# Two instead of three pairs of plain column tiles in each ConvFFN of a hybrid decoder trunk

## The chip, the cores and the metric

The kernel runs on one core of one Trainium2 chip. The metric is the device time of one execution in microseconds (us). The core has five engines that run side by side, each with its own queue worked off in order: TensorE (PE, matrix products; weight loads are shown as PEld), VectorE (DVE), ScalarE (ACT), GpSimd (POOL) and SyncE (SP, which here only issues transfers). They wait for one another by semaphores. Products land in eight PSUM banks, and DVE or ACT must take them out before a bank is used again.

## The reference

One step of a two-layer decoder trunk for 1024 prompt tokens and 8 x 8 sample tokens, 1088 columns in all, with 1024 channels. Layer 0 mixes tokens by sliding-window attention, layer 1 by a gated spatial MLP. Each layer ends with a ConvFFN, and this is what the change touches:

```
def conv_ffn(h, past, w_up, conv_w, conv_b, w_down):
    T = h.shape[1]
    a = h @ w_up
    ap = jnp.concatenate([past.astype(a.dtype), a], 1)
    conv = sum(conv_w[j] * ap[:, j:j + T] for j in range(CONV_W)) + conv_b
    g, u = jnp.split(conv, 2, axis=-1)
    y = (jax.nn.silu(g) * u) @ w_down
    return y, ap[:, T:]
```

Here h is the normalised and modulated input (1024 channels), w_up has 2 x 2816 columns, which are 2 x 22 tiles of 128, and each gate tile j belongs with the up tile 22 + j.

## The kernel before, in words

Activations are kept with channels on partitions and tokens along the row. Every float32 operand is split into a high part, rounded to the fast matmul type, and the remainder, so that a product needs three matmuls: high by high, high by low, low by high. The 1088 tokens lie in two halves h of 544, each of which has a first part of 272 (z = 0) and a second (z = 1).

**The norm** (class Norm4, line 1415) makes h in tiles `hf`, one for each z, group g of four channel blocks, and parity b. Lines 1450 and 1451 split them into `ha` and `hb` (16 tiles for the whole input). `sums` (line 1456) makes, for each of the four groups (z, g) in `todo`, the four block sums that the seven-product scheme needs, in four DVE instructions (lines 1459 to 1462) into two tiles `T`, after which the two `hf` tiles are free. `split` (line 1465) splits the two `T` into two `th` (ACT, line 1469) and two `tl` (DVE, line 1470).

**Plain columns.** For the first NCV = 3 pairs of column tiles (gate j and up 22 + j) the kernel takes plain products: `u_conv` (line 1654) and `u_step` (line 1512) run 8 channel blocks x 3 matmuls x 2 halves = 48 matmuls of 272 columns for each tile and z. They read `ha` and `hb` only, so PE has work while the sums are made. The first two columns start within the last block of the projection before (`last_block7`, line 1536), which also calls the weight splitter `ws.split` six times (lines 1554 and 1572); for a plain column that is an ACT cast (line 309) and a DVE subtraction (line 316) into two of the eight weight buffers, for raw weights of a seven-product pair only the load (lines 299 to 302). In `ffn` (line 1782) the second halves of three columns run interleaved while the norm's second part is applied (lines 1855 to 1860); the fourth column's follows, and the fifth and sixth run whole, in the loop at line 1869.

**Seven-product pairs.** The other 19 pairs use a Strassen-Winograd scheme over 2 x 2 blocks (channel parity by gate/up side against channel parity by token half): seven products in the order 1, 2, 4, 6, 5, 7, 3 (`pair`, line 1659), each 12 matmuls for each z, and DVE additions of the results (lines 1674 to 1704). Products 1, 2 and 3 read `ha` and `hb`; 4 to 7 read the split sums `th` and `tl`. `pair_weights` (line 1612) prepares the seven weights: each is an ACT cast (line 1621) and a POOL subtraction (line 1622); weights 1, 2 and 4 come straight from the raw blocks, 6 and 5 from the sums `Sa` (POOL, lines 1629 and 1632), 7 and 3 from `Sb` (lines 1636 and 1639). For the first pair, two steps of this (GA = 2) come ahead of the last plain half and the rest follow.

**Convolution and gate.** `conv` (line 1804) is one ACT pass (line 1807) and two DVE passes (lines 1808 and 1810) over 1104 columns into a tile `cv`; the last columns are saved by ACT for plain columns and by POOL for the others (lines 1812 to 1817). `gate` (line 1820) is ACT's SiLU, two DVE products (lines 1823 and 1824), a POOL copy (line 1825), and a store on ACT's queue.

**What sets the order.** The attention part is ordered by hand; from line 1187 on the framework's planner orders each engine's queue when the program is built: an instruction goes in when its inputs are ready by the planner's own estimate of times, earlier code first. Most large tiles come from one pool of 37 slots (NSLOT), and an instruction whose tile gets no slot waits. Weights have eight buffers, raw weights two.

In the loop over the plain columns n (tile n // 2, gate or up by n % 2), the work beside PE's is, in the order of the code: take out the column, convolve it, split whatever was summed, at n = 0 and 2 sum another group, at odd n the gate of the pair. Two groups are summed ahead of the loop, and the first of them is split there.

Of the kernel before, what the change touches and what calls it, by code (L numbers as in the profile page):

```python
# [33 lines left out]
GA, GB = 2, 0  # L34
STEPS = {4: (0, 2), 6: (1, 3), 7: (4, 6)}
RA, RB, RC = 0, 1, 7
NCV = 3
SLOT = 1106
SH1, SC1, G1, SH2, SC2, G2 = range(6)
ORD = (0, 2, 1, 3, 4, 6, 5, 7)  # L40
# [27 lines left out]
def plan():  # L68
# [25 lines left out]
    def ffn(l):  # L94
        r = []
        for j in range(NJ):
            if j < NCV:
                r += [(("up", l, j), 1024), (("up", l, NJ + j), 1024)]
# [242 lines left out]
def build(nc, tc, a, ctx):  # L341
# [15 lines left out]
    def banks(n, name="b"):  # L357
        return [bank(name) for _ in range(n)]
# [184 lines left out]
    with ExitStack() as p1:  # L543
# [102 lines left out]
        un2, yb, todo, done = [], {}, {}, []  # L646
# [965 lines left out]
    def pair_weights():  # L1612

        (_, l, j), r1, _ = ws.take("ua")
        r2 = ws.take("ub")[1]
        A11, A21, A12, A22 = r1[:, 0:512], r1[:, 512:1024], r2[:, 0:512], r2[:, 512:1024]
        W = {}

        def parts(i, src, eng=G):
            t = wp.tile([128, 1024], F32R, name="w7", tag="w")  # L1620
            A.copy(t[:, 0:512], src)  # L1621
            eng.tensor_sub(t[:, 512:1024], src, t[:, 0:512].bitcast(F32))  # L1622
            W[i] = t
        yield W
        parts(1, A11)
        yield
        parts(2, A12)
        sa = slot([128, 2, 512], name="Sa")
        G.tensor_add(sa[:, 0, :], A21, A22)
        yield  # L1630
        parts(4, A22)
        G.tensor_sub(sa[:, 1, :], sa[:, 0, :], A11)  # L1632
        yield
        parts(6, sa[:, 1, :])
        sb = slot([128, 2, 512], name="Sb")
        G.tensor_sub(sb[:, 0, :], A11, A21)
        yield
        parts(5, sa[:, 0, :])
        G.tensor_sub(sb[:, 1, :], A12, sa[:, 1, :])
        yield  # L1640
        del r1, r2, A11, A12, A21, A22, sa
        parts(7, sb[:, 0, :])
        yield
        parts(3, sb[:, 1, :])
        del sb
        yield
# [7 lines left out]
    def u_conv(norm, w, z, ps):  # L1654

        for k in ORD:
            u_step(norm, w, z, ps, k, k == 0, k == 7)
# [124 lines left out]
    def ffn(l, norm, nxt):  # L1782
# [6 lines left out]
        def ext(jj):  # L1789
            e = slot([128, 1106], name="ext")  # L1790
            es = e[:, 1026:1106].rearrange("p (b t) -> p b t", t=10)
            G.memset(e[:, 0:2], 0.0)
            G.tensor_copy(es[:, :, 0:2], past[:, jj])
            return e
# [9 lines left out]
        def conv(e, jj):  # L1804
            es = e[:, 1026:1106].rearrange("p (b t) -> p b t", t=10)
            t = slot([128, 1106], name="cv")
            A.activation(t[:, 0:1104], e[:, 2:1106], AF.Identity, scale=cw(jj * 3 + 2), bias=cb(jj))  # L1807
            V.scalar_tensor_tensor(t[:, 0:1104], e[:, 1:1105], cw(jj * 3 + 1), t[:, 0:1104],  # L1808
                                   op0=ALU.mult, op1=ALU.add)
            V.scalar_tensor_tensor(t[:, 0:1104], e[:, 0:1104], cw(jj * 3), t[:, 0:1104],  # L1810
                                   op0=ALU.mult, op1=ALU.add)
            if jj % NJ < NCV:
                A.copy(past[:, jj], es[:, :, 8:10])
                A.copy(stp[:, jj, :], e[:, 1024:1026])
            else:
                G.tensor_copy(past[:, jj], es[:, :, 8:10])
                G.tensor_copy(stp[:, jj, :], e[:, 1024:1026])
            return t

        def gate(j, tg, tu):  # L1820
            A.activation(tg[:, 0:1104], tg[:, 0:1104], AF.Silu)
            sv = [q[:, 1026:1106].rearrange("p (b t) -> p b t", t=10)[:, :, 0:8] for q in (tg, tu)]
            V.tensor_mul(tg[:, 0:SEQ], tg[:, 0:SEQ], tu[:, 0:SEQ])  # L1823
            V.tensor_mul(v88(tu[:, 0:64]), sv[0], sv[1])
            G.tensor_copy(tg[:, SEQ:T], tu[:, 0:64])
            A.dma_start(ps_scr[j], tg[:, 0:T])


        def evac(e, ps, z):
            for h in range(2):  # L1830
                for o, f in places(e, h, z):
                    A.copy(o, f(ps[h]))

        todo = [(z, g) for z in range(2) for g in range(2)]
# [25 lines left out]
                    u_step(norm, un[n], 1, bk[n], k, k == 0, k == 7)  # L1860
        w = un[3]
        un = None
        for g_ in range(2):
            norm.sums(*todo[0], V)
            taken.append(todo.pop(0))
            if not g_:
                norm.split(*taken.pop(0))
        ts = []
        for n in range(2 * NCV):
            jj = n % 2 * NJ + n // 2  # L1870
            if n < 3:
                e, ps = es[n], bk[n]
                es[n] = bk[n] = None
            else:
                if n == 3:
                    e = es.pop()
                else:
                    w = ws.take("up")[1:]
                    ps = banks(2, "u")
                    e = ext(jj)  # L1880
                    u_conv(norm, w, 0, ps)
                    evac(e, ps, 0)
                if n == 2 * NCV - 1:
                    gen = pair_weights()
                    W = next(gen)
                    for _ in range(GA):
                        next(gen)
                ps = banks(2, "u")
                u_conv(norm, w, 1, ps)
                if n == 2 * NCV - 1:  # L1890
                    for _ in range(GB):
                        next(gen)
                w = None
            evac(e, ps, 1)
            del ps
            ts.append(conv(e, jj))
            del e
            if n >= 2 and n < 2 * NCV - 2:
                ws.ahead(2)
            while taken:  # L1900
                norm.split(*taken.pop(0))
            if todo and n % 2 == 0:
                norm.sums(*todo[0], V)
                taken.append(todo.pop(0))
            if n % 2 == 1:
                gate(n // 2, *ts)
                ts = []
# [29 lines left out]
        return nn  # L1937

    norm = ffn(0, norm, lambda: Norm7(None, None, paired=True))


# [33 lines left out]
    todo = [(z, q) for z in range(2) for q in range(4)]  # L1975
# [155 lines left out]
    norm = Norm4(mods[1, SC2], mods[1, SH2])  # L2131
    down.run(norm, {LA: lambda: rest(0), LB: lambda: rest(1)})
    norm = ffn(1, norm, Norm)
    norm.finish()

# [27 lines left out]
```

## Time and profile before

| | |
|---|---|
| time, median of 3 runs | 2590.87 us (2586.61 to 2592.92) |
| the profiled execution's own time | 2589.49 us |
| its span, first to last instruction | 2587.7 us |
| mean granted TensorE clock | 0.994 |
| first ConvFFN: second half of the fourth plain column starts | 488.36 us |
| first ConvFFN: first seven-product pair starts | 518.47 us |
| matmuls | 17916 |

The profile is one execution. A row of the timeline reads: start in us, duration in us, engine, line of the code, operation, output <- inputs, shapes, how many instructions were merged into the row, and in square brackets how long the engine had been idle before and what released it. A row of the table of stages reads: the stretch, its length, busy us of PE, PEld, DVE, ACT and POOL with their instruction counts, then the granted clock (1.00 is full speed) and the transfers. Matmuls are pipelined: one of 272 columns lasts 0.288 us in the rows, but the next starts about 0.125 us after it.

### The profile page before, as it was taken

What the parts mean: (1) busy time and instruction counts of PE and PEld (TensorE: products, weight loads), DVE (VectorE), ACT (ScalarE), POOL (GpSimd) and SP (SyncE); (2) the same over time, 40 slices, a digit from 0 to 9 for tenths busy, and PEclk for the clock granted to TensorE, in tenths of its full rate; (3) what the DMA queues carried; (4) which work ended last, traced back from release to release, by engine and by line L of the source; (5) the groups of instructions that cost most, each with busy time, mean ns of one, the idle gap of its engine ahead of it and who ended that gap; (6) DMA issues with size and microseconds to landing.
All of it is one profiled execution on the core that took longest, in us unless ns stands there. A gap on an engine that the chain in (4) does not pass through costs nothing.

```text
span 2587.7 us, 45783 instructions
## 1 busy us (share of the span) xinstructions
PE 2535.6 (98%) x17916; PEld 2373.8 (92%) x17916; DVE 1616.8 (62%) x3254; ACT 982.6 (38%) x1939; POOL 1240.9 (48%) x1392
## 2 busy tenths in 40 slices
PE   7999999999999999999999999999999999999998
PEld 4667789999999999999788999999999999999998
DVE  5416866767767764456744555655687766676545
ACT  3216854533334331114325655212553333332203
POOL 2325631399999900001643755212179999940003
PEclk9999999999999999999999999999999999999999
DMA  8342214022222275453322534522112222254211
GB/s 302 102 153 100 74 57 139 10 80 81 85 81 76 93 288 181 159 187 127 91 84 76 169 127 156 200 99 74 66 59 76 76 80 79 77 192 158 89 45 70
DMA packets 113943, 292.20 MB, mean 113 GB/s; under 512 B 15328, under 2 KB 47136, under 8 KB 113696
## 3 DMA queue, kind: packets, MB, share of 16 engines
q1 hardware_dynamic: 82016, 232.49, 27.4%
q10 hardware_dynamic: 31712, 56.79, 5.8%
q8 instruction: 142, 2.33, 0.4%
q14 instruction: 73, 0.60, 0.1%
HBM read 228.06 MB, written 63.07 MB: 113 GB/s over the span
## 4 chain that ended last, share of the span: by engine, by line
PE 86%; DVE 6%; ACT 3%; POOL 2%; DMA 2%; issue 1%; SPq 0%; ACTq 0%; DVEq 0%; POOLq 0%
PE m L375 32%; PE acc L375 23%; PE misc L375 9%; PE v L375 7%; PE y L375 5%; PE u L375 5%; PE adaps L375 1%; POOL w L1622 1%; DMA raw<-wts 1%; ACT P L841 1%; PE rs L375 1%; DVE cv L1823 1%; PE pv L375 1%; DVE cv L1810 1%; PE sc L375 1%
## 5 line engine op out<-in xcount | busy, mean ns | idle before, releaser
L375 PE MATMUL m<-th,w 128*128 128x272 f32 x2944 | 562.6, 288 | 6.4 <-DVE ext L1676 6.3
L375 PEld LDWEIGHTS m<-th,w 128*128 128x128 f32 x2944 | 466.2, 188 | 7.0 <-issue 6.6
L375 PE MATMUL m<-tl,w 128*128 128x272 f32 x1472 | 424.9, 289 | 0.0
L536 DVE SCALAR_TENSOR_TENSOR x<-acc,mod,x 128x384 f32<-128x384 f32 (+1 forms) x312 | 159.6, 567 | 237.6 <-PE acc L375 232.0
L375 PE MATMUL m<-hb,w 128*128 128x272 f32 x2208 | 294.3, 289 | 0.0
L375 PEld LDWEIGHTS m<-hb,w 128*128 128x128 f32 x2208 | 285.1, 190 | 0.0
L375 PEld LDWEIGHTS m<-tl,w 128*128 128x128 f32 x1472 | 277.5, 189 | 0.0
L375 PE MATMUL acc<-gh,whi 128*128 128x384 f32 (+1 forms) x1152 | 255.9, 330 | 1.1 <-DVE mixed L2089 0.8
L375 PE MATMUL acc<-gl,whi 128*128 128x384 f32 (+1 forms) x1152 | 253.6, 328 | 0.6 <-DVE gl L1729 0.6
L375 PE MATMUL acc<-gh,wlo 128*128 128x384 f32 (+1 forms) x1152 | 253.2, 327 | 0.0
L309 ACT CAST whi<-raw 128x1024 fp32r<-128x1024 f32 (+1 forms) x108 | 109.7, 1017 | 377.9 <-PE acc L375 230.5
L1622 POOL TENSOR_TENSOR w<-raw,w 128x512 fp32r<-128x512 f32 x138 | 194.5, 1422 | 82.2 <-ACT w L1621 76.0
L375 PEld LDWEIGHTS acc<-gh,whi 128*128 128x128 f32 x1152 | 194.7, 188 | 10.2 <-issue 6.2
L375 PEld LDWEIGHTS acc<-gl,whi 128*128 128x128 f32 x1152 | 195.6, 188 | 0.9 <-DVE gl L1729 0.9
L1808 DVE SCALAR_TENSOR_TENSOR cv<-ext,cst,cv 128x1104 f32<-128x1104 f32 x88 | 125.4, 1460 | 112.9 <-ACT cv L1807 53.9
L375 PEld LDWEIGHTS acc<-gh,wlo 128*128 128x128 f32 x1152 | 195.7, 188 | 0.0
L1621 ACT CAST w<-Sa 128x512 fp32r<-128x512 f32 x92 | 56.8, 622 | 307.9 <-POOL Sa L1632 162.0
L1676 DVE TENSOR_TENSOR ext<-ev,m 128x272 f32<-128x272 f32 (+1 forms) x456 | 137.5, 338 | 47.6 <-PE m L375 39.3
L1303 POOL TENSOR_TENSOR nsq<-nsq 128x544 f32<-128x544 f32 x18 | 24.9, 1385 | 273.4 <-ACT nsq L1296 273.4
L1810 DVE SCALAR_TENSOR_TENSOR cv<-ext,cst,cv 128x1104 f32<-128x1104 f32 x88 | 155.6, 1802 | 0.1
L375 PE MATMUL m<-ha,w 128*128 128x272 f32 x1104 | 146.6, 289 | 0.0
L375 PEld LDWEIGHTS m<-ha,w 128*128 128x128 f32 x1104 | 141.2, 188 | 0.6
(293 smaller groups left out, 5506.8 us busy)
## 6 DMA issues: line engine op xcount, KB each, us to landing
raw<-wts SPq DMA_DIRECT2D x238, 512.0 KB, 4.0
wada<-wts SPq DMA_DIRECT2D x54, 512.0 KB, 4.3
pscr<-cv ACTq DMA_DIRECT2D x44, 544.0 KB, 5.5
p<-pscr SPq DMA_DIRECT2D x40, 544.0 KB, 5.5
xscr<-x ACTq DMA_DIRECT2D x24, 512.0 KB, 2.8
x<-xscr SPq DMA_DIRECT2D x24, 512.0 KB, 8.3
sscr<-mixed ACTq DMA_DIRECT2D x16, 544.0 KB, 3.5
vscr<-v ACTq DMA_DIRECT2D x32, 256.0 KB, 2.6
```

What stands on the lines that cost most here:

```text
L309: nc.scalar.copy(hi[:, :c], r[:, :c])
L375: PE.matmul(out, lhsT=l, rhs=r, start=start, stop=stop)
L536: V.scalar_tensor_tensor(xv, p[:, 0:w], gp, xv, op0=ALU.mult, op1=ALU.add)
L841: A.activation(p, p, AF.Exp, bias=nm[:, h:h + 1], scale=0.125, accum_out=su[:, h:h + 1])
L1303: (V if z or m == 7 else G).tensor_add(s.ss[z], s.ss[z], q)
L1621: A.copy(t[:, 0:512], src)
L1622: eng.tensor_sub(t[:, 512:1024], src, t[:, 0:512].bitcast(F32))
L1676: V.tensor_add(o, f(p), f(q))
L1808: V.scalar_tensor_tensor(t[:, 0:1104], e[:, 1:1105], cw(jj * 3 + 1), t[:, 0:1104], op0=ALU.mult, op1=ALU.add)
L1810: V.scalar_tensor_tensor(t[:, 0:1104], e[:, 0:1104], cw(jj * 3), t[:, 0:1104], op0=ALU.mult, op1=ALU.add)
L1823: V.tensor_mul(tg[:, 0:SEQ], tg[:, 0:SEQ], tu[:, 0:SEQ])
```

## The change

NCV goes from 3 to 2, so that plain products make the first two pairs of column tiles and the seven-product scheme the other 20. Of the four groups of block sums, three instead of two are summed ahead of the loop, and the first two instead of the first are split there. Within the loop, the one that is left is summed after n = 1 instead of after n = 0 and n = 2. The order of the weights in memory, `plan` (line 68), follows NCV.

```
-NCV = 3
+NCV = 2
...
-        for g_ in range(2):
+        for g_ in range(3):
             norm.sums(*todo[0], V)
             taken.append(todo.pop(0))
-            if not g_:
+            if g_ < 2:
                 norm.split(*taken.pop(0))
         ts = []
         for n in range(2 * NCV):
...
             while taken:
                 norm.split(*taken.pop(0))
-            if todo and n % 2 == 0:
+            if todo and n % 2 == 1:
                 norm.sums(*todo[0], V)
                 taken.append(todo.pop(0))
             if n % 2 == 1:
                 gate(n // 2, *ts)
```

With NCV = 2 the loop has four columns, all of which have been started before it; the weights of the first pair are prepared at n = 3.

More of the change, by code (lines that the diff above doesn't have):

```diff
@@ L36 @@
 RA, RB, RC = 0, 1, 7
-NCV = 3
+NCV = 2
 SLOT = 1106
@@ L1862, in ffn @@
         un = None
-        for g_ in range(2):
+        for g_ in range(3):
             norm.sums(*todo[0], V)
             taken.append(todo.pop(0))
-            if not g_:
+            if g_ < 2:
                 norm.split(*taken.pop(0))
@@ L1901, in ffn @@
                 norm.split(*taken.pop(0))
-            if todo and n % 2 == 0:
+            if todo and n % 2 == 1:
                 norm.sums(*todo[0], V)
```

## The prediction

> **What bounds the kernel now.** I read the page's busy times first, then the table of stages around the first ConvFFN, then the queues of TensorE (PE), VectorE (DVE), ScalarE (ACT) and GpSimd (POOL) in order of time. The second ConvFFN runs the same way 1386.2 us later (the last two rows below, its first block sum), so one is worked out and doubled.
>
> ```profile
> span 2587.7 us, 45783 instructions
> PE 2535.6 (98%) x17916; PEld 2373.8 (92%) x17916; DVE 1616.8 (62%) x3254; ACT 982.6 (38%) x1939; POOL 1240.9 (48%) x1392
> 427.00:455.00 28.00, 24.40 (x168) 23.50 (x168) 20.52 (x49) 13.43 (x26) 0.00 (x0) 0.88 0.45 150
> 455.00:488.40 33.40, 33.40 (x267) 33.37 (x268) 19.29 (x28) 16.46 (x34) 6.49 (x17) 1.00 0.01 1
> 488.40:518.40 30.00, 30.00 (x241) 30.00 (x241) 28.96 (x25) 21.20 (x45) 13.89 (x10) 1.00 0.05 20
> 518.40:539.50 21.10, 21.10 (x170) 21.10 (x170) 16.37 (x24) 8.00 (x18) 19.50 (x18) 1.00 0.27 89
> 602.70:630.00 27.30, 24.57 (x183) 24.38 (x183) 19.07 (x26) 10.87 (x17) 27.22 (x30) 0.94 0.36 110
> 470.88 0.72 DVE L1459 TENSOR_TENSOR T<-hf 128x544 f32<-128x544 f32 x1
> 1857.06 0.72 DVE L1459 TENSOR_TENSOR T<-hf 128x544 f32<-128x544 f32 x1
> ```
>
> The columns after the stage and its length are busy us of PE, weight loads, DVE, ACT and POOL, then the granted clock and the DMA. PE is the bound: it never pauses from 455 to 602.7. But in the stretch where the plain columns end (488.4 to 518.4) DVE is also 97% busy, and in the pair stretch POOL is 92%. That is the stretch the change shortens.
>
> ```profile
> 488.36 0.67 PE L375 MATMUL u<-ha,whi 128*128 128x272 f32 x4
> 518.47 3.19 PE L375 MATMUL m<-ha,w 128*128 128x272 f32 x24
> 524.51 0.29 PE L375 MATMUL m<-th,w 128*128 128x272 f32 x1
> 539.54 3.18 PE L375 MATMUL m<-ha,w 128*128 128x272 f32 x24
> ```
>
> Row 488.36 starts the second half of the fourth plain column, 518.47 the first seven-product pair, 524.51 its third product (i=4, the first that reads the split block sums), 539.54 the next pair.
>
> **The change part by part.**
>
> *TensorE.* Removed per ConvFFN: one pair of plain columns, 2 columns x 2 halves x 48 = 192 matmuls. Added: one seven-product pair, 7 x 2 x 12 = 168. A pair takes 539.54 - 518.47 = 21.07 us, or 0.1254 us a matmul, so 24 fewer are worth 3.0 us; 6.0 us for both ConvFFNs, 0.23% of the time. Even whole, this is under the 0.3% (7.8 us) that a measurement of this kernel can tell from no change. The added pair also brings POOL some 19.5 us of work and DVE 16.4 (row 518.4); both are under PE's 21.07, so the pairs that follow stay PE's.
>
> *The block ahead.* The last block of the preceding projection calls the weight splitter six times. Now only four of the six find a plain column; the fifth and sixth find raw weights of the first pair and issue only the load. Gone there are two ACT casts and two DVE subtractions, and one cast stands in front of a wait of PE:
>
> ```profile
> 443.30 1.04 ACT L309 CAST whi<-raw 128x1024 fp32r<-128x1024 f32 x1 [1.48 <-PE misc L375]
> 445.20 1.22 DVE L316 TENSOR_TENSOR wlo<-raw,whi 128x1024 fp32r<-128x1024 f32 x1
> 445.49 0.53 PE L375 MATMUL u<-ha,whl 128*128 128x272 f32 x2 [1.98 <-ACT ha L1450]
> 446.82 0.82 PE L375 MATMUL u<-ha,whl 128*128 128x272 f32 x2 [0.81 <-ACT ha L1450]
> 449.27 4.49 PE L375 MATMUL u<-ha,whl 128*128 128x272 f32 x20
> 492.63 0.68 ACT L1621 CAST w<-raw 128x512 fp32r<-128x512 f32 x1
> ```
>
> The weight buffer that the cast waited for now goes to a cast of the first pair's weights. The planner does pull those forward: row 492.63 is one, though the code has it after the sixth column's first half. So I exchange 1.04 for 0.68 and take 0.4 us. Bounds: 0; and 2.79 us (both waits) plus what 20 matmuls took over 20 x 0.1254 there, 4.49 - 2.51 = 1.98, so 4.8.
>
> *Sums and splits.* The third group's sum and the second group's split move ahead of the first convolution, where DVE has a hole:
>
> ```profile
> 478.03 0.72 DVE L1462 TENSOR_TENSOR T<-hf,T 128x544 f32<-128x544 f32 x1
> 489.15 1.37 DVE L1808 SCALAR_TENSOR_TENSOR cv<-ext,cst,cv 128x1104 f32<-128x1104 f32 x1 [10.39 <-ACT cv L1807]
> 490.44 1.29 DVE L1470 TENSOR_TENSOR tl<-T,th 128x1088 fp32r<-128x1088 f32 x1
> 491.64 1.37 DVE L1810 SCALAR_TENSOR_TENSOR cv<-ext,cst,cv 128x1104 f32<-128x1104 f32 x1
> 492.92 1.29 DVE L1470 TENSOR_TENSOR tl<-T,th 128x1088 fp32r<-128x1088 f32 x1
> 503.84 2.31 DVE L1823 TENSOR_TENSOR cv<-cv 128x1024 f32<-128x1024 f32 x1
> 506.07 1.35 DVE L1808 SCALAR_TENSOR_TENSOR cv<-ext,cst,cv 128x1104 f32<-128x1104 f32 x1
> 508.77 0.75 DVE L1459 TENSOR_TENSOR T<-hf 128x544 f32<-128x544 f32 x1
> 511.77 1.37 DVE L1808 SCALAR_TENSOR_TENSOR cv<-ext,cst,cv 128x1104 f32<-128x1104 f32 x1 [0.22 <-ACT cv L1807]
> 515.55 1.28 DVE L1470 TENSOR_TENSOR tl<-T,th 128x1088 fp32r<-128x1088 f32 x1
> ```
>
> A split costs two tl of 1.2 us (start to start), a sum 2.8 us (508.77 to 511.77, less the idle 0.22): 5.2 us into a hole of 10.39. Free, if slots suffice: 16 tiles of the norm, 4 columns, 4 weight parts, 8 split sums, 2 sums and 2 unsummed ones are 36 of the 37. Otherwise the sum falls behind 489.15 and adds 2.8 to the next step.
>
> *The fourth group.* It is still summed between convolutions, after the second, and split after the third. The first convolution cannot start earlier, since 488.36 does not move. But the first pair moves from 518.47 to 488.36 + 48 x 0.1254 = 494.4, 24.1 us earlier. Its i=4 product then starts at 524.51 - 24.1 = 500.4, and wants the fourth group in the last quarter, 18 matmuls later, at 502.7. DVE's list from 489.15 until that split is done: three convolutions of 2.6 (489.15 to 490.44 and 491.64 to 492.92), two splits of 2.4, the sum 2.8, the first gate product 2.2 (503.84 to 506.07): 17.6 us, so 506.8, with no waits. The old list (four convolutions, three splits, two sums, one gate product, 25.4 us) took 27.7 us to 516.83, so waits of up to 2.3 come on top. PE waits 4.1 to 6.4 us; I take 5. If the planner put the split ahead of the gate product and the third convolution (4.8 us), nothing would be left; the rows show it following the code.
>
> *Weights of the first pair.* The first three weights read raw data and can be made ahead, in the gap that POOL has. The next four need the sums Sa and Sb, which take slots:
>
> ```profile
> 493.39 3.87 POOL L1622 TENSOR_TENSOR w<-raw,w 128x512 fp32r<-128x512 f32 x1 [30.24 <-ACT w L1621]
> 515.79 2.18 POOL L1629 TENSOR_TENSOR Sa<-raw 128x512 f32<-128x512 f32 x1 [2.59 <-DVE cv L1810]
> 518.05 2.15 POOL L1632 TENSOR_TENSOR Sa<-Sa,raw 128x512 f32<-128x512 f32 x1
> 523.11 1.30 POOL L1622 TENSOR_TENSOR w<-Sa,w 128x512 fp32r<-128x512 f32 x1 [1.45 <-ACT w L1621]
> 530.58 3.56 POOL L1622 TENSOR_TENSOR w<-Sb,w 128x512 fp32r<-128x512 f32 x2
> raw<-wts SPq DMA_DIRECT2D x238, 512.0 KB, 4.0
> ```
>
> POOL stood idle for 30 us with slots free and raw weights landed, yet Sa began only 0.24 us after the last tl (515.55). I read this as slots being handed out in code order, so the new Sa starts near 506, behind the fourth split. Its first weight was done 8.6 us after it (524.41), the third some 16.6. PE wants them at 503.4 + 5 = 508.4 and 6 us later, so it waits a further 6.2 to 8.2 us. If Sa is placed in the hole instead, 0. I take 4, about the middle, since part of the 8.6 us (2.9 between Sa's end at 520.2 and the weight) is waiting on the second gate, which now comes later. Queued behind Sa on POOL are the gate copies and the new columns' headers; ACT's casts wait with them, and the convolutions wait on those. On SP's queue the first pair's two loads move ahead by the two plain columns' place; they land in 4.0 us (last row), long before use, and only further weight loads stand behind them: nothing.
>
> [...]
>
> *The clock.* PE's present waits in the pairs show what a pause costs besides its length:
>
> ```profile
> 622.40 0.37 PE L375 MATMUL m<-th,w 128*128 128x272 f32 x1 [2.73 <-DVE ext L1676]
> 1988.33 0.36 PE L375 MATMUL m<-th,w 128*128 128x272 f32 x1 [3.52 <-DVE ext L1676]
> 1989.00:1990.00 1.00, 1.00 (x7) 1.00 (x6) 0.92 (x3) 0.00 (x0) 1.00 (x2) 0.56 0.00 0
> 1990.00:1991.00 1.00, 1.00 (x7) 1.00 (x6) 0.97 (x3) 0.00 (x0) 1.00 (x3) 0.50 0.00 0
> ```
>
> In the stage from 602.7, 183 matmuls at 0.1254 are 22.9 us against 24.6 busy: 1.6 us lost to the half clock. I take this once per ConvFFN, the two waits being close together; bounds 0 and 3.2. [...]
>
> *Sum.* Per ConvFFN -3.0 - 0.4 + 5 + 4 + 1.6 = +7.2 us; twice, +14.4. The profiled execution took 2589.49 us (span 2587.7 and 1.8 around it), 1.4 under the median of 2590.87. On the median: 2605.3.
>
> **The rivals.** *A, all hidden:* the planner fits the fourth split and Sa in time; -3.4 twice, 2584.1, within 0.3%. For it: the hole of 10.39 us and POOL's 30. Against it: 17.6 us of DVE work for a window of 13.5 (489.15 to 502.7). It decides from the point where the fourth split ends by 502.7 and Sa starts by 492.8 (16.6 before the seventh product's 509.4).
>
> *B, the later wait goes too:* the waits at 622.40 and 1988.33 come once in each ConvFFN, when POOL and DVE, starting late, overtake PE. If the new wait resets that phase, 2.73 + 3.52 + 2 x 1.6 = 9.5 us come back: 2595.8, also within 0.3%. Nothing in the rows decides for or against.
>
> *C, faster:* A, and the cast at 443.30 was the real holder of PE's 1.98 and 0.81; with it gone these waits and the slow 20 matmuls vanish, 4.8 twice: 2590.87 - 6.0 - 9.6 = 2575.3. For it: the chain of waits runs through that cast. Against: a weight cast takes its buffer and place.
>
> **How the numbers follow.** The forecast gets 0.53, A 0.25, B 0.09, C 0.13. Hence faster 0.13, within 0.3% 0.34, slower 0.53. The top comes from the unknown costs at their bounds: 6.4 + 8.2 + 3.2 - 3.0 = 14.8 twice is 2620.5; I stop at 2619. Below, the range takes in A: 2583. C and the far top are left out. The forecast's own range is 2599 to 2619.
>
> **What the new profile should show.** 48 fewer matmuls in all. Two block sums' splits and three sums before the first L1808. First pair near 494.4 on this trace's clock. If I am right, PE m waits on DVE tl L1470 for about 5 us in its third product, then on POOL w L1622, with the clock near 0.5 after. Wrong: no PE wait between 494 and 516; Sa before 495; or PE's waits at 445 gone.

## The result and the profile after

| | before | after |
|---|---|---|
| median of 6 runs each, one chip | 2591.45 us (2586.61 to 2594.43) | 2604.95 us (2600.27 to 2606.29) |
| ratio after to before | | 1.0052, 95% interval 1.0039 to 1.0065 |
| the profiled execution's own time | 2589.49 us | 2606.29 us |
| matmuls | 17916 | 17868 |

The changed kernel is slower by 0.52%. First the busy times on the page of after, then its table of stages (stage, length, busy us of PE, PEld, DVE, ACT and POOL, clock, transfers): the block ahead, the plain columns, the last plain half, the first pair, the second pair, and the stretch where the old wait at 622.40 stood.

```profile
PE 2538.1 (97%) x17868; PEld 2373.9 (91%) x17868; DVE 1622.7 (62%) x3286; ACT 983.3 (38%) x1921; POOL 1270.7 (49%) x1422
```

```profile
426.75:457.00 30.25, 26.60 (x171) 25.46 (x172) 20.09 (x46) 12.99 (x26) 4.29 (x3) 0.83 0.26 98
457.00:489.86 32.86, 32.86 (x263) 32.86 (x263) 24.41 (x34) 18.36 (x36) 6.48 (x17) 1.00 0.00 1
489.86:495.88 6.02, 6.02 (x50) 6.02 (x49) 5.23 (x5) 6.00 (x18) 0.00 (x0) 1.00 0.01 3
495.88:529.97 34.09, 25.36 (x170) 24.29 (x169) 23.19 (x32) 15.46 (x26) 27.69 (x22) 0.80 0.20 73
529.97:551.02 21.05, 21.05 (x171) 21.05 (x170) 13.78 (x24) 7.46 (x12) 20.97 (x22) 1.00 0.23 64
610.00:640.00 30.00, 29.74 (x238) 29.55 (x238) 24.82 (x37) 13.84 (x21) 29.74 (x35) 1.00 0.31 91
```

The plain columns run without a pause, as before. The first pair takes 34.09 us where a pair takes 21.05, with PE busy for only 25.36 of them and the clock at 0.80. The stretch from 610, where before lost 2.73 us and clock, is now almost whole: one pause of 0.26 us is left in it. PE's rows in order of time:

```profile
437.73 1.90 PE L375 MATMUL u<-hb,whl 128*128 128x272 f32 x13 [1.15 <-DVE hb L1451]
445.88 0.82 PE L375 MATMUL u<-ha,whl 128*128 128x272 f32 x2 [1.98 <-ACT ha L1450]
447.05 2.86 PE L375 MATMUL u<-ha,whl 128*128 128x272 f32 x11 [0.36 <-DVE ha L1451]
495.88 3.18 PE L375 MATMUL m<-ha,w 128*128 128x272 f32 x24
506.20 0.39 PE L375 MATMUL m<-th,w 128*128 128x272 f32 x1 [1.90 <-ACT th L1469]
508.17 0.59 PE L375 MATMUL m<-tl,w 128*128 128x272 f32 x1 [1.58 <-DVE tl L1470]
512.24 0.60 PE L375 MATMUL m<-th,w 128*128 128x272 f32 x1 [2.57 <-ACT w L1621]
516.42 0.82 PE L375 MATMUL m<-th,w 128*128 128x272 f32 x2 [2.68 <-POOL w L1622]
```

So the first pair waits first for the fourth group's split (1.90 + 1.58), then for weights made from Sa (2.57 + 2.68): 8.73 us. It is 34.09 - 21.07 = 13.02 us longer than a pair; the other 4.3 are nearly all the half clock. What the two waits had in front of them, on VectorE and GpSimd of the same execution:

```profile
484.61 0.73 DVE L1462 TENSOR_TENSOR T<-hf,T 128x544 f32<-128x544 f32 x1
490.65 1.37 DVE L1808 SCALAR_TENSOR_TENSOR cv<-ext,cst,cv 128x1104 f32<-128x1104 f32 x1 [5.32 <-ACT cv L1807]
506.18 1.93 DVE L1470 TENSOR_TENSOR tl<-T,th 128x1088 fp32r<-128x1088 f32 x1 [0.34 <-ACT th L1469]
502.21 2.44 POOL L1825 COPY cv<-cv 128x64 f32<-128x64 f32 x1 [37.65 <-DVE cv L1824]
504.62 2.34 POOL L1629 TENSOR_TENSOR Sa<-raw 128x512 f32<-128x512 f32 x1
515.11 2.49 POOL L1622 TENSOR_TENSOR w<-Sa,w 128x512 fp32r<-128x512 f32 x2
```

The three sums and two splits ended at 485.3, in the hole as forecast (5.32 us of it were left over). The last tl ended at 508.1. Sa began at 504.62, right behind the gate's copy and before that tl had begun, and the subtractions for its weights ran from 515.11 on.

The second ConvFFN shows the same four waits. The start of the down projection (its first `acc` row) dates what each ConvFFN brought; before, then after:

```profile
923.70 0.67 PE L375 MATMUL acc<-gh,whi 128*128 128x384 f32 x3
2310.14 0.98 PE L375 MATMUL acc<-gh,whi 128*128 128x384 f32 x3
```

```profile
930.09 0.51 PE L375 MATMUL acc<-gh,whi 128*128 128x384 f32 x2
2324.88 0.34 PE L375 MATMUL acc<-gh,whi 128*128 128x384 f32 x1
```

The lead-in, taken from the first u matmul of the block ahead to the first pair less 24.08 us (192 x 0.1254) for a third plain pair, went from 66.74 to 69.13 and in the second ConvFFN from 65.51 to 69.52. With that, each term is measured:

| us, first and second ConvFFN | forecast | measured |
|---|---|---|
| 24 matmuls fewer | -3.0 | -3.0, -3.0 |
| block ahead (lead-in) | -0.4 | +2.4, +4.0 |
| waits in the first pair | +5 and +4 | +8.7, +8.8 |
| half clock in it | +1.6 | +4.3, +4.5 |
| later wait at the turn of the pairs | 0 (rival B: -4.8) | -5.1, -6.3 |
| sum | +7.2 | +7.3, +8.0 |

The last row but one is what is left between the second pair's start and the down projection. The two sums make 15.3 us. The two profiled executions, from which the table is taken, lie 16.8 us apart, the medians 13.5; the profiled execution of after is the longest of its six.

### The profile page after: what moved, and what is told of

Its sections match the earlier page's. It is cut to its first block, busy times and chain, and to the rows that moved or that the text cites. A ratio compares the mean times of both kernels' runs of the same rounds, so it can differ in the third digit from the quotient of the medians.

```text
span 2604.5 us, 45746 instructions
## 1 busy us (share of the span) xinstructions
PE 2538.1 (97%) x17868; PEld 2373.9 (91%) x17868; DVE 1622.7 (62%) x3286; ACT 983.3 (38%) x1921; POOL 1270.7 (49%) x1422
## 3 DMA queue, kind: packets, MB, share of 16 engines
q8 instruction: 142, 2.33, 0.4%
## 4 chain that ended last, share of the span: by engine, by line
PE 84%; DVE 5%; POOL 4%; issue 2%; ACT 2%; DMA 1%; SPq 0%; DVEq 0%; POOLq 0%; ACTq 0%
PE m L375 32%; PE acc L375 23%; PE misc L375 9%; PE v L375 7%; PE y L375 5%; PE u L375 3%; POOL w L1622 2%; PE adaps L375 2%; PE rs L375 1%; ACT P L841 1%; DMA p<-pscr 1%; DMA raw<-wts 1%; PE pv L375 1%; PE sc L375 1%; PE tp L891 0%
## 5 line engine op out<-in xcount | busy, mean ns | idle before, releaser
L375 PE MATMUL m<-th,w 128*128 128x272 f32 x3072 | 593.1, 290 | 14.6 <-POOL w L1622 5.4
L375 PEld LDWEIGHTS m<-th,w 128*128 128x128 f32 x3072 | 489.8, 190 | 16.5 <-POOL w L1622 6.0
L375 PE MATMUL m<-tl,w 128*128 128x272 f32 x1536 | 445.1, 290 | 3.1 <-DVE tl L1470 3.1
L375 PE MATMUL m<-hb,w 128*128 128x272 f32 x2304 | 304.2, 288 | 0.0
L375 PEld LDWEIGHTS m<-tl,w 128*128 128x128 f32 x1536 | 292.3, 190 | 3.6 <-DVE tl L1470 3.6
L375 PEld LDWEIGHTS m<-hb,w 128*128 128x128 f32 x2304 | 294.5, 188 | 0.0
L1676 DVE TENSOR_TENSOR ext<-ev,m 128x272 f32<-128x272 f32 (+1 forms) x480 | 144.7, 337 | 49.7 <-PE m L375 40.1
L1808 DVE SCALAR_TENSOR_TENSOR cv<-ext,cst,cv 128x1104 f32<-128x1104 f32 x88 | 125.7, 1465 | 68.1 <-issue 39.2
L1810 DVE SCALAR_TENSOR_TENSOR cv<-ext,cst,cv 128x1104 f32<-128x1104 f32 x88 | 159.4, 1846 | 0.0
L375 PE MATMUL m<-ha,w 128*128 128x272 f32 x1152 | 152.3, 288 | 0.0
L375 PEld LDWEIGHTS m<-ha,w 128*128 128x128 f32 x1152 | 146.8, 188 | 0.6
```

Source lines behind the costliest of these rows:

```text
L375: PE.matmul(out, lhsT=l, rhs=r, start=start, stop=stop)
L1676: V.tensor_add(o, f(p), f(q))
```

## The experiments

Times are medians beside the kernel before on the same chip (2587.3 to 2590.0 in the four groups of runs); the ratios are those to compare.

**The first part alone.** Two pairs of plain columns, sums as before.

```
-        for g_ in range(3):
+        for g_ in range(2):
...
-            if g_ < 2:
+            if not g_:
...
-            if todo and n % 2 == 1:
+            if todo and n % 2 == 0:
```

> The changed kernel with its second part undone: two pairs of plain columns, but the block sums as before (two groups summed ahead, one of them split there, the third and fourth summed after n = 0 and n = 2). My theory, that the first pair waits for the fourth group's split and for Sa behind it: a sum of 2.8 us and a split of 2.4 come back into VectorE's window, and the fourth sum comes one convolution later, so the first wait grows by about 5.2 us per ConvFFN and what stands behind it moves with it: about 2615 us, with the wait of TensorE on tl or th in the first pair near 8.7 us instead of 3.5. Rival 1, the weights from Sa set the time alone: the later split hides beneath their wait, 2605 to 2608 us. Rival 2, the sums moved ahead are what disturbs the block ahead: about 2600 us.

2613.56 us, ratio 1.0092 (1.0075 to 1.0110). PE's waits in the first pair:

```profile
510.28 0.59 PE L375 MATMUL m<-th,w 128*128 128x272 f32 x1 [7.26 <-ACT w L1621]
511.94 1.05 PE L375 MATMUL m<-th,w 128*128 128x272 f32 x3 [0.84 <-POOL w L1622]
519.95 0.59 PE L375 MATMUL m<-tl,w 128*128 128x272 f32 x1 [4.47 <-DVE tl L1470]
```

The size came as my theory had it, with the order of the two waits exchanged: the weights first, then the later split. From the start of the first pair to the down projection this kernel takes 5.1 and 6.2 us more than the changed one; the theory had 5.2. Both rivals are out. At the turn of the pairs only 0.20 us was left in one of the two ConvFFNs, though the sums were late: a long wait in the first pair also takes that wait away.

**The second part alone.** Three pairs of plain columns; the inverse edit, on the kernel before.

> The kernel before with the second part alone: three pairs of plain columns, three groups summed and two split ahead of the loop, the fourth summed after n = 1. My theory: the moved work lies in VectorE's hole, TensorE does not wait at that place in either kernel, so 2591 us within 4. Rival 1: the wait at the turn of the first pairs (2.73 and 3.52 us, and 1.6 of half clock each) comes of VectorE's late start and goes with the earlier sums: about 2582 us. Rival 2: the earlier sums hold slots that the new columns need, and the columns start late: 2595 us or more, with waits of TensorE in the plain columns.

2583.14 us, ratio 0.9977 (0.9967 to 0.9987): faster than both kernels, and rival 1 was right. The stage in which before lost its 2.73 us, here:

```profile
600.00:630.00 30.00, 30.00 (x240) 29.86 (x240) 24.71 (x33) 14.09 (x22) 29.92 (x30) 1.00 0.29 91
```

PE has no pause from 455 to 660, and the wait is gone in the second ConvFFN too. The earlier sums move VectorE's backlog into its hole, and with three plain pairs this alone removes the wait. The two parts by themselves give +23.6 and -6.8 us, together +16.8; the change measured +13.5, and the interval of the first part alone is 4.5 us wide to either side.

**Weight buffers held.** In the block ahead the planner had put three casts and three subtractions of the first pair's weights, here on GpSimd's queue after the change:

```profile
433.94 3.02 POOL L1622 TENSOR_TENSOR w<-raw,w 128x512 fp32r<-128x512 f32 x2 [24.61 <-ACT w L1621]
444.38 1.27 POOL L1622 TENSOR_TENSOR w<-raw,w 128x512 fp32r<-128x512 f32 x1 [7.42 <-ACT w L1621]
```

In this run four dummy tiles hold the buffers until the first block sum.

```
             norm.sums(*todo[0], V)
+            for i in range(0 if g_ else 4):
+                hold = wp.tile([128, 1024], F32, name="hold", tag="w")
+                G.tensor_copy(hold[:, 0:1], norm.tt[0, 0][i % 2][:, 0, 0, 0:1])
```

> The changed kernel with four weight buffers held until the first block sum is there, so that the first pair's weights 1, 2 and 4 cannot be made within the block ahead (four one-column GpSimd copies are added). My theory: the 2.4 to 2.8 us that the block ahead lost in each ConvFFN come from these casts and subtractions, and come back: about 2600 us, with the second half of the fourth plain column near 487.4 instead of 489.9, the waits of 1.15 and 0.36 us on hb and ha gone and the subtractions of line 1622 near 472. The first pair's waits stay, since Sa's place does not change. Rival 1: the order of TensorE's matmuls there, not the weights, made the loss: 2605 us. Rival 2: the weights are then late for the first pair: 2607 us or more, with waits on w in products 1 to 4.

2598.68 us, ratio 1.0032 (1.0017 to 1.0048): 5 us less than the changed kernel by the ratios, 6.3 by the medians. The wait of 1.15 us on hb is gone, and the first pair is unchanged (34.32 us). VectorE's queue shows where that wait came from. In the changed kernel these two rows run beside the GpSimd subtraction at 433.94, ahead of the hb subtraction that PE waits for:

```profile
434.32 1.49 DVE L1432 SCALAR_TENSOR_TENSOR hf<-x,mod,rsb 128x544 f32<-128x544 f32 x1
435.74 1.30 DVE L1534 TENSOR_TENSOR xs<-xs,gs 128x64 f32<-128x64 f32 x1
```

In the kernel before they take 0.78 and 0.22 us, with the buffers held 0.77 and 0.22.

The lead-in was 67.93 and 64.96. Over all runs with two plain pairs it averages 65.1 in the five kernels with held buffers and 68.2 in the five without, 3.1 us apart. Only about half of this is the weights' own price; the other half is the clock. In each of the fourteen traces the granted clock changes only at marks that lie 3.41 us apart, and a lead-in has from none to three such steps at half clock. Without held buffers it takes 65.6 us with none, 68.1 with two and 69.1 to 69.5 with three; with held buffers 63.7 to 63.8, 66.4 to 66.5 and 67.9. At the same number of half-clock steps the two kinds are 1.2 to 1.9 us apart.

The number of steps depends on where the marks fall. The run of the first part alone had the weights pulled forward too, and waits of 1.15, 1.98 and 0.66 us, but no half clock in the block: its lead-in is 65.56 and 65.55. Two steps each around the wait of 1.98 us (after, then the first part alone):

```profile
442.41:445.82 3.41, 1.49 (x12) 1.26 (x11) 2.01 (x5) 1.75 (x3) 1.27 (x1) 1.00 0.00 0
445.82:449.24 3.42, 3.01 (x11) 2.69 (x12) 3.23 (x6) 1.43 (x4) 0.00 (x0) 0.50 0.37 153
```

```profile
444.17:447.58 3.41, 1.98 (x16) 1.76 (x15) 1.51 (x5) 1.25 (x3) 0.94 (x1) 1.00 0.01 5
447.58:450.99 3.41, 2.20 (x15) 1.93 (x15) 3.36 (x6) 1.93 (x4) 0.33 (x1) 1.00 0.37 154
```

In the first the wait lies all but wholly within one step, PE is idle for 1.93 us of that step, and the clock is half from the next mark on. In the second a mark divides the wait into 1.43 and 1.21 us of idle time, the next pause included, and the clock stays whole. The +2.4 and +4.0 us of the table, with three half-clock steps each, thus hold some luck of this one execution.

**The gate's store on SyncE.** In the execution after, the store of the first gate stood on ScalarE's queue ahead of the last th cast.

```
-            A.dma_start(ps_scr[j], tg[:, 0:T])
+            (SP if j < NCV else A).dma_start(ps_scr[j], tg[:, 0:T])
```

> The changed kernel with the gate's store of the plain pairs issued by SyncE instead of ScalarE; the planned order of TensorE, VectorE and GpSimd is the same. Looks at what the store did that stood between the two th casts of the fourth group (504.68) and waited for GpSimd's copy. My theory: the second cast goes some 1.6 us earlier and TensorE's first waits (1.90 and 1.58 us) shrink by that, but Sa begins behind the same GpSimd copy at 504.6, so the wait on the weights grows by as much: 2603 to 2605 us. Rival: Sa and the weights follow the split, and the whole chain moves up: 2599 us or less.

2604.75 us, ratio 1.0053 (1.0037 to 1.0069): no change, but not as my theory had it. Its PE wait, and what VectorE did before:

```profile
513.05 0.59 PE L375 MATMUL m<-tl,w 128*128 128x272 f32 x1 [3.74 <-DVE tl L1470]
```

```profile
509.36 1.36 DVE L1810 SCALAR_TENSOR_TENSOR cv<-ext,cst,cv 128x1104 f32<-128x1104 f32 x1
510.64 2.36 DVE L1470 TENSOR_TENSOR tl<-T,th 128x1088 fp32r<-128x1088 f32 x1
```

The wait on th is gone, and the one on tl is about as long as both were together (3.74 against 3.48). VectorE has no gap ahead of that tl, so its list sets the wait, not the store.

**The fourth split ahead of the gate.**

```
+            while n == 1 and taken:
+                norm.split(*taken.pop(0))
             if n % 2 == 1:
                 gate(n // 2, *ts)
```

> The changed kernel with the fourth group's split moved ahead of the first gate (code order; the planner now puts it ahead on VectorE and ScalarE, and puts Sa ahead of the gate's GpSimd copy). The gate product (2.31 us) and the store then no longer stand before the last tl. My theory: the waits on th and tl (1.90 + 1.58) go to under 1 us, Sa begins some 3 us earlier because its slot comes behind the split, and the waits on the weights stay at about 5, so some 3 to 4 us in each ConvFFN: 2597 to 2599 us. Rival 1: the gate product was not what delayed the split, the waits stay and so does the time: 2605 us. Rival 2: without the first wait TensorE only reaches the wait on the weights earlier, which grows by as much: 2603 to 2605 us.

2604.83 us, ratio 1.0058 (1.0044 to 1.0073). Rival 2:

```profile
511.56 0.59 PE L375 MATMUL m<-th,w 128*128 128x272 f32 x1 [5.54 <-ACT w L1621]
516.93 0.82 PE L375 MATMUL m<-th,w 128*128 128x272 f32 x2 [4.56 <-POOL w L1622]
```

```profile
500.30 5.90 POOL L1629 TENSOR_TENSOR Sa<-raw 128x512 f32<-128x512 f32 x1 [35.14 <-ACT ev L1687]
```

No wait on the split is left. Sa began 3.8 us behind the start of the first pair instead of 8.7, but is shown with 5.90 us beside a full VectorE (the profile's page calls GpSimd's spans rough). The subtractions for its weights began only 1.1 us sooner, counted in the same way, and the two waits on w are 10.1 us.

**Sa early.** The weight steps ahead of the loop (GA = 4, so that Sa and Sb ask for their slots earlier).

```
-GA, GB = 2, 0
+GA, GB = 4, 0
...
+        gen = pair_weights()
+        W = next(gen)
+        for _ in range(GA):
+            next(gen)
         ts = []
         for n in range(2 * NCV):
...
-                if n == 2 * NCV - 1:
-                    gen = pair_weights()
-                    W = next(gen)
-                    for _ in range(GA):
-                        next(gen)
```

> The changed kernel with the first pair's weight steps taken ahead of the loop over the plain columns (four of them, so both halves of Sa and the first of Sb get their slots earlier in code order; GpSimd's planned order has them before the first gate copy). My theory, that the weights are late only because Sa's slots are handed out in code order: the waits of 2.57 and 2.68 us on w go, the wait on th and tl stays at about 3.5, and some of the half clock goes: 2592 to 2595 us. [...] Rival 2: the slots that Sa takes are missed by the sums or columns, TensorE waits in the plain columns: over 2605 us.

2596.76 us, ratio 1.0025 (1.0015 to 1.0035), 1.8 us above my range. Sa now runs in the hole, and the first pair has lost its waits on weights:

```profile
485.71 1.70 POOL L1629 TENSOR_TENSOR Sa<-raw 128x512 f32<-128x512 f32 x1 [18.19 <-DVE tl L1470]
```

```profile
510.86 0.82 PE L375 MATMUL m<-th,w 128*128 128x272 f32 x2 [2.46 <-ACT th L1469]
542.64 0.36 PE L375 MATMUL m<-th,w 128*128 128x272 f32 x1 [1.46 <-DVE ext L1676]
586.02 0.36 PE L375 MATMUL m<-th,w 128*128 128x272 f32 x1 [1.07 <-DVE ext L1676]
```

That Sa came late because of its place in the code is shown. Whether its slot or its place in GpSimd's planned queue held it is not told apart, since this edit moves both. The first pair takes 25.65 us instead of 34.09, but waits on ext have come back in later pairs.

**All three.** Held buffers, early Sa, split before the gate.

> The changed kernel with all three: weight buffers held over the block ahead, weight steps ahead of the loop, the fourth split before the first gate. My theory says that nothing is left of the first pair's waits and of the block's loss, so that this is the kernel before with the sums alone (2583.1) less 48 matmuls at 0.1254: 2577 us, TensorE without a wait of over 0.5 us between 455 and 640. Rival 1: the remaining wait on th and tl (about 3 us with its clock in each ConvFFN) stays: 2583 us. [...]

2598.17 us, ratio 1.0032 (1.0020 to 1.0044): not the 2577 that my theory gave.

```profile
507.99 0.60 PE L375 MATMUL m<-th,w 128*128 128x272 f32 x1 [6.19 <-ACT th L1469]
522.82 0.36 PE L375 MATMUL m<-th,w 128*128 128x272 f32 x1 [2.77 <-DVE ext L1676]
```

```profile
475.10 1.82 DVE L1459 TENSOR_TENSOR T<-hf 128x544 f32<-128x544 f32 x1
497.25 1.82 DVE L1459 TENSOR_TENSOR T<-hf 128x544 f32<-128x544 f32 x1
```

With the weights' GpSimd work in VectorE's hole, single instructions of a sum take 1.82 us instead of 0.72 (a GpSimd subtraction runs beside each of the two above), and the fourth sum ends at 506.8, where the changed kernel had it done at 501.9.

**Four pairs of plain columns**, sums as in the second part alone (NCV = 4).

> Four pairs of plain columns, with the sums as in the run with the sums alone (2583.1 us); 48 more matmuls than that. My theory: with the first seven-product pair later, nothing waits, and TensorE's count alone speaks: 48 x 0.1254 = 6.0 us more, 2589 us. Rival: VectorE and GpSimd gain from the plain pair (about 16 and 19 us of work less each) and some wait that is still there goes: 2583 us or less. Other rival: more work stands in the plain columns (two more convolutions and a gate) and TensorE waits there: over 2592 us.

2587.88 us, ratio 0.9994 (0.9984 to 1.0004), 0.0017 or 4.4 us above three pairs with the same sums; the 6.0 that TensorE's count gives lies within the two intervals. No wait of PE stands in the pairs of either, and the count is the price here.

**All four sums ahead of the loop**, buffers held; then the same with Sa early; then three plain pairs with four sums ahead.

```
-        for g_ in range(3):
+        for g_ in range(4):
```

> The changed kernel with the weight buffers held over the block ahead and all four groups summed ahead of the loop; the split of the third and fourth comes after the first convolution. In the run with all three mends the fourth sum stood among convolutions and the gate product (497.25 to 506.09) while VectorE had been idle for 3.88 us before them; here it goes into that idle time, and the planned order puts the fourth split ahead of the second convolution. My theory: the fourth split ends near 500, before TensorE wants it, and no wait on th or tl is left; Sa still gets its slot only behind it in code order, near 500 too, so some wait on w in the products 6 and 5 stays (up to 5 us and its clock): 2583 to 2592 us beside a kernel before of 2590. Rival 1: TensorE reaches the weights earlier and waits there for as long as before in all: 2598 us, as with the buffers held alone. Rival 2: the convolutions that are put back by the splits come too late for the gates and the next pair's slots: waits on ext appear in the second pair, 2598 us or more.

> The same with the first pair's weight steps taken ahead of the loop as well. My theory says that now nothing is left to wait for in the first pair: the kernel with the sums alone (0.9977 of the kernel before) less 48 matmuls at 0.1254: 2578 us beside a kernel before of 2590, and no wait of TensorE over 0.5 us between 455 and 640. [...] Rival 2: a backlog of VectorE behind the first pair turns into waits on ext in the second pair (2.77 us in the run with all three mends): 2583 to 2588 us.

> The kernel before, three pairs of plain columns, with all four groups summed ahead of the loop. Tells whether earlier sums go on paying where the first pair is not short of time. My theory: the waits at the turn of the pairs are gone already with three groups ahead, so 0.9977 of the kernel before again, 2584 us beside 2590. Rival: slots held by the fourth group's sums delay a column: 2590 us or more, with a wait of TensorE between 490 and 515.

2598.48 us, ratio 1.0039 (1.0025 to 1.0053); 2600.21 us, 1.0044 (1.0028 to 1.0059); 2582.02 us, 0.9979 (0.9968 to 0.9989). With three plain pairs my theory held. With two it did not. In the first of these the pauses are scattered over the first pair (0.70, 0.23, 1.97, 0.99, 1.50 us), then a backlog shows as 3.48 in the third, and as 4.12 in the second pair of the second ConvFFN:

```profile
503.85:516.88 13.03, 8.33 (x59) 7.48 (x59) 13.03 (x12) 3.96 (x7) 13.03 (x10) 1.00 0.18 55
```

```profile
562.73 0.36 PE L375 MATMUL m<-th,w 128*128 128x272 f32 x1 [3.48 <-DVE ext L1676]
```

VectorE and GpSimd are busy for every one of those 13.03 us. With Sa early as well the waits move again, the longest to 3.58 us, and 4.74 in the second ConvFFN:

```profile
502.10 0.39 PE L375 MATMUL m<-th,w 128*128 128x272 f32 x1 [1.65 <-ACT th L1469]
517.03 0.60 PE L375 MATMUL m<-th,w 128*128 128x272 f32 x1 [3.58 <-DVE ext L1676]
```

**Less work for VectorE.** The kernel with four sums ahead, Sa early and buffers held, with line 1810 left out for the plain columns. It leaves out one of the three taps there, so it tells only of time.

```
-            V.scalar_tensor_tensor(t[:, 0:1104], e[:, 0:1104], cw(jj * 3), t[:, 0:1104],
-                                   op0=ALU.mult, op1=ALU.add)
+            if jj % NJ >= NCV:
+                V.scalar_tensor_tensor(t[:, 0:1104], e[:, 0:1104], cw(jj * 3), t[:, 0:1104],
+                                       op0=ALU.mult, op1=ALU.add)
```

> The kernel with four sums ahead, weight steps ahead and buffers held, with the second VectorE pass of the convolution (line 1810) left out for the four plain columns of each ConvFFN: 4 x 1.3 us of VectorE's work less, so those columns are convolved with two taps instead of three. Every reordering so far moved TensorE's waits of 6 to 9 us in the first two pairs without removing them. My theory: with two pairs of plain columns TensorE's time there is too short for VectorE's list, whatever its order; with 5.2 us less of it the waits on ext (3.58 and 4.74 us) and the one on tl go, a wait on th that comes of ScalarE's casts (1.65 us) may stay: 2580 to 2588 us beside a kernel before of 2588, that is 12 or more less than the same kernel with the pass. [...]

2594.79 us, ratio 1.0024 (1.0014 to 1.0034): about 5 us less, not 12 or more, so my theory does not hold as put. The waits on tl and ext did go, but others opened, and VectorE itself now stood idle for ScalarE:

```profile
504.34 0.59 PE L375 MATMUL m<-th,w 128*128 128x272 f32 x1 [3.38 <-ACT ext L1833]
514.79 0.59 PE L375 MATMUL m<-th,w 128*128 128x272 f32 x1 [2.68 <-ACT ev L1687]
```

```profile
503.99 1.37 DVE L1808 SCALAR_TENSOR_TENSOR cv<-ext,cst,cv 128x1104 f32<-128x1104 f32 x1 [2.41 <-ACT cv L1807]
513.46 1.97 DVE L1824 TENSOR_TENSOR cv<-cv 128x1024 f32<-128x1024 f32 x1 [3.05 <-ACT cv L1822]
```

ScalarE's queue took VectorE's place in these waits; that the planner's new order of its casts, copies and stores did this was not tried. Which of amount and order decides for two plain pairs stays open.

## Why the prediction was right

The median of 2604.95 lies 0.35 us from the 2605.3 forecast, but so close a hit is luck. By the table of terms the block ahead was forecast 2.8 and 4.4 us too low and the clock 2.7 and 2.9 too low, while the later wait, 5.1 and 6.3 us, was not expected to go; these errors cancel. What was right is the mechanism of the two waits in the first pair and their size.

*Right with mechanism and size.* The 24 matmuls (-3.0). The sums and the second split in the hole. The fourth split, late for the third product: from the first convolution to its end VectorE's list was summed as 17.6 us and took 17.5 (490.65 to 508.1), with none of the waits of up to 2.3 us that might have come on top, so PE waited 3.5 us, a little under the 4.1 to 6.4 of the forecast. The store on ScalarE's queue, which the new profile shows ahead of the last th cast, did not set that wait.

*Right in size, with part of the reason wrong.* Sa was forecast near 506 and began at 504.62, and the run with Sa early shows that its place in the code is the reason. But it did not stand behind the fourth split: it stood behind the gate's copy on GpSimd and began before the last tl. The row at 515.79 in the prediction already names a convolution pass (L1810) as what released Sa, not the tl beside it. The wait on the weights was 5.2 us where the forecast took 4, the middle between 0 and 8.2, so its nearness is partly luck. Both waits together are 8.7 us against 9.

*The clock, mis-sized.* The forecast took 1.6 us once per ConvFFN from the wait at 622.40, with a bound of 3.2. It was 4.3 and 4.5, above the bound: four pauses within 12 us kept the clock at half in between, from 507.26 to 520.92.

*The block ahead, wrong in sign.* The step failed at "I exchange 1.04 for 0.68": three casts, not one, came into the block, with their three GpSimd subtractions, which the forecast left out there, though it named them for the gap behind. VectorE's work beside those subtractions took longer (1.49 us instead of 0.78 and 1.30 instead of 0.22), and a new wait of 1.15 us came. The prediction's own rows have a subtraction of 3.87 us at 493.39, with VectorE busy for 3.82 us beside it, and one of 1.30 at 523.11, with VectorE idle; the forecast made nothing of that for the block ahead. With the half clock the block cost +2.4 and +4.0 us. The run with held buffers gives the wait back.

*Rival B came true beside the forecast.* I gave it 0.09 as a case of its own, with "nothing in the rows decides for or against". The run with the sums alone shows that the moved sums remove the wait at the turn by themselves; the run of the first part alone shows that the new wait does so too, but for 0.20 us. The row of VectorE's 10.39 idle us ahead of 27.7 full ones was where to see it. It is the step that missed most: the second part was costed at nothing and is worth -6.8 us with three plain pairs.

Rivals A and C are out: the split did not fit in, and PE's 1.98 us at 445 stayed with the cast at 443.30 gone, even in the run with held buffers, where no weight cast stands in its place.

## What to carry to other kernels

When a bounding engine gets less work, ask first what else had to be finished under that work: here TensorE saved 3.0 us in each ConvFFN, but the first pair came some 23 us earlier, in a stretch where VectorE had no time to spare. Holding the buffers and asking for Sa early each won back part of the loss (5 and 7 us); every further mend only moved the wait, in the end to another engine. An edit that only fills an idle stretch of a second engine can be worth more than the edit beside it; time the parts singly. Count a planner's freedom as part of the change: here the freed weight buffers were filled in an earlier stage, where nobody had looked for a cost.

## What the runs showed of the hardware

Pauses of the same length did not always cost the same, and the marks of the clock tell why. In all fourteen traces every stretch at half clock, but for the last one that the end of the trace cuts off, lasts 3.41, 6.83, 10.24 or 13.65 us: one to four steps of 3.41. Counted by these steps, from the block ahead to the down projection of both ConvFFNs, the clock went from whole to half 48 times. In 45 of them PE had been idle for 1.93 us or more of the step before; the other three had 1.28, 1.60 and 1.77. Of the steps at whole clock after which it stayed whole, none had more than 1.84 us idle, and none with 1.27 or less was followed by half clock. In between both came up. At half clock idle time was not needed for it to go on: in the execution after, PE was busy for all of 449.24 to 452.65 at half clock, and the step behind it stood at half as well.

So a pause of 1.98 us halved the clock where it lay within one step and not where a mark divided it, and the five pauses of the run with four sums ahead (0.23 to 1.97 us within 13 us), which come to 0.70 to 1.50 us in each step, left it whole. In the first pair of the changed kernel no pause exceeds 2.68 us, but four steps in a row hold 2.57, 1.91, 1.91 and 2.33 us, and the stage stands at 0.80. The marks lie differently against the program in each execution: the same wait of 1.98 us ended 0.06 us behind a mark in the execution after, 0.56 in the first part alone and 2.60 in the kernel before. With the same waits a lead-in then took from 65.6 to 69.5 us.

Where VectorE and GpSimd worked at the same time, instructions of both were often longer. An instruction of a block sum took 1.82 us with a GpSimd subtraction beside it (the run with all three) and 0.72 without. Half of Sa took 2.34 us at 504.62, with VectorE busy for 2.00 of them, and 1.28 at 521.28, with VectorE busy for 0.40. The row at 435.74 took 1.30 us beside a subtraction; the run with held buffers has no GpSimd subtraction there, and it took 0.22 again. It was not so each time: the convolution pass at 504.47 (L1810) took 1.36 us beside Sa, as long as the one at 493.13 with GpSimd idle. That this is also why earlier weights paid only in part is my reading.
